# Seven block products accumulated in shared PSUM banks, and layer 1's last MLP quarter in the same form with weight sums formed by adding transfers

## The chip, the cores and the metric

The kernel runs on one core of a Trainium2 chip. The metric is the device time of one execution in microseconds, as the median of several runs. The engines are named as in the profile: PE (TensorE: matmuls; its weight loads stand as PEld), DVE (VectorE), ACT (ScalarE), POOL (GpSimd) and SP (SyncE, which here only issues transfers).

## The reference

Two layers over 512 tokens of width 1024 in float32. Each has three sub-layers of the form x <- LayerNorm(alpha * x + f(x)): a token mixer (mLSTM in layer 0, causal pooling in layer 1), cross-attention into 256 memory tokens, and the MLP, which is what the change touches:

```python
def sq_relu_mlp(x, w1, b1, w2, b2):
    return jnp.square(jax.nn.relu(x @ w1 + b1)) @ w2 + b2      # 1024 -> 4096 -> 1024

for i in range(DEPTH):                                          # DEPTH = 2
    ...
    x = layer_norm(ALPHA * x + sq_relu_mlp(x, mlp_w1[i], mlp_b1[i], mlp_w2[i], mlp_b2[i]),
                   ln_g[i, 2], ln_b[i, 2])
```

## The kernel before

Every float32 operand of a matmul is split in two parts, a high one (a cast on ACT to the format that PE takes) and a low one (the rest, a subtraction on DVE); a product is three matmuls, high by high, high by low and low by high (`mm3`, L196 to L199). Tiles of weights are 128x1024 (512 KB); a matmul is 128x512.

The MLP goes through its 4096 hidden units in four quarters q of 1024. A quarter has a hidden phase (8 tiles of 128 hidden units, 24 matmuls each, then bias, relu and square on ACT) and a down-projection that adds to x, which lies in SBUF as four tiles of 128 tokens by 1024.

For q = 0, 1, 2 (`up_down`) the down-projection is a 2x2 block product by seven products instead of eight. The squared activations are four blocks: a11, a12 for tokens 0 to 255 and a21, a22 for tokens 256 to 511, where the second figure says which half of the quarter's hidden units (a11 and a21 are hidden tiles 0 to 3, a12 and a22 tiles 4 to 7). The weights are b11, b12, b21, b22 in the same way. Sums and differences of blocks are made on DVE (`each` L839 for weights; L845, L869, L873 and one more for activations), then split (L777/L778 activations, L786/L787 weights). A product (`product`) is two groups of 12 matmuls, each into its own PSUM bank of 128x512, 24 in all. The order is M1, M7, M5, M2, M6, P3, P4. M1, M5, M6 and M7 are needed in more than one block of the result: `into` gathers them over q = 0, 1, 2 in two SBUF tiles (`sums`; an ACT copy for q = 0, a DVE add at L852 for the others). M2, P3 and P4 are added to x at once (L859).

For q = 3 the product is direct (`down`): 8 groups of 24 matmuls, 192. In the middle of its hidden phase `gather` (L882 to L893) adds the sums to x, with 16 DVE adds of 128x512. In layer 1 each token tile gets its LayerNorm as soon as its second half is added: statistics (L241), aggregate (L246), a square root on ACT, a reciprocal, four scalar_tensor_tensor (L253, L254), and two transfers to the output.

What runs when: the order of instructions on each engine is fixed when the program is built, by the order of the code, the pools' buffers and the framework's scheduling, and each engine takes its own queue in order, waiting where an operand isn't there. All loads of weights go through SP's queue. Those for the seven products go to a pool of six buffers (`rawd`), so a load waits until an earlier tile of the pool is done with. GpSimd has nothing to do after layer 0's mixer.

Of the kernel before, what the change touches and what calls it, by code (L numbers as in the profile page):

```python
# [15 lines left out]
P = 128  # L16
# [27 lines left out]
def trunk(ctx: ExitStack, tc: tile.TileContext, a: dict, out: bass.AP):  # L44
# [151 lines left out]
    def mm3(out_, l, r, start, stop):  # L196
        T.matmul(out_, l[0], r[0], start=start, stop=False)  # L197
        T.matmul(out_, l[0], r[1], start=False, stop=False)  # L198
        T.matmul(out_, l[1], r[0], start=False, stop=stop)  # L199
        if later:  # L200
            tick(3 * max(r[0].shape[-1], 128) / 2400)
# [451 lines left out]
    for i in range(DEPTH):  # L653
# [137 lines left out]
        def product(name, lhs, rhs, evac):  # L791

            for g in range(2):
                ps = acc_p.tile([P, 512], F32, tag="acc", name=f"{name}{g}")
                for k in range(4):
                    w = rhs[k // 2]
                    mm3(ps, tuple(z[:, k, tok(g)] for z in lhs), (w[0][:, k % 2], w[1][:, k % 2]), start=k == 0, stop=k == 3)
                evac(g, ps)

        sums = {}  # L800

        def up_down(q, n):

# [11 lines left out]
            if q == 0:  # L815
# [7 lines left out]
                for z in "ab":  # L823
                    sums[z] = act_p.tile([P, 2, 2, 512], F32, tag="act", name=f"sum{i}{z}")
                sums["M1"], sums["M6"] = sums["a"][:, 0], sums["a"][:, 1]
                sums["M5"], sums["M7"] = sums["b"][:, 0], sums["b"][:, 1]
# [4 lines left out]
            def load(name, hf, j):  # L831
                z = [scoped["rawd"].tile([P, WU], F32, tag="rawd", name=f"{name}{n}{z}") for z in range(2)]
                for w in range(2):
                    ld(z[w], a["w2"][i, q, hf, j + w])
                return z
# [11 lines left out]
            def into(key):  # L847
                def evac(g, ps):
                    if q == 0:
                        A.copy(sums[key][:, g], ps)  # L850
                    else:
                        V.tensor_tensor(sums[key][:, g], sums[key][:, g], ps, ALU.add)  # L852

                return evac

            def onto(row, hf):
                def evac(g, ps):
                    z = x[2 * row + g][:, hf_cols(hf)]
                    V.tensor_tensor(z, z, ps, ALU.add)  # L859

                return evac

            b11 = load("b11", 0, 0)
            product(f"m1{n}", L["M1"], weight_split(f"b11{n}", b11), into("M1"))
            b12, b22 = load("b12", 1, 0), load("b22", 1, 2)
            each(b11, b11, b12, ALU.add)
            each(b12, b12, b22, ALU.add)
            product(f"m7{n}", L["M7"], weight_split(f"t3{n}", b12), into("M7"))
            V.tensor_tensor(a21, a21, a22, ALU.subtract)  # L869
            product(f"m5{n}", split(f"q1{n}", a21), weight_split(f"t1{n}", b11), into("M5"))  # L870
            b21 = load("b21", 0, 2)
            product(f"m2{n}", split(f"a12{n}", a12), weight_split(f"b21{n}", b21), onto(0, 0))
            V.scalar_tensor_tensor(a11, a11, -1.0, a22, ALU.mult, ALU.subtract)  # L873
            each(b11, b11, b22, ALU.add)
            product(f"m6{n}", split(f"q2{n}", a11), weight_split(f"t2{n}", b11), into("M6"))
            V.tensor_tensor(a12, a12, a11, ALU.add)
            product(f"p3{n}", split(f"q4{n}", a12), weight_split(f"b22{n}", b22), onto(0, 1))
            each(b11, b11, b21, ALU.add)
            product(f"p4{n}", split(f"a22{n}", a22), weight_split(f"t4{n}", b11), onto(1, 0))

        def gather():

            for g in range(2):
                u, w, f, m7 = (sums[z][:, g] for z in ("M1", "M6", "M5", "M7"))
                x11, x12, x21, x22 = (x[2 * r + g][:, hf_cols(c)] for r in range(2) for c in range(2))
                V.tensor_tensor(x11, x11, u, ALU.add)
                V.tensor_tensor(u, u, w, ALU.add)
                V.tensor_tensor(x12, x12, f, ALU.add)
                V.tensor_tensor(x12, x12, u, ALU.subtract)
                V.tensor_tensor(u, u, m7, ALU.add)  # L890
                V.tensor_tensor(x21, x21, u, ALU.add)
                V.tensor_tensor(x22, x22, f, ALU.add)
                V.tensor_tensor(x22, x22, u, ALU.subtract)  # L893

        for q in range(3):
            up_down(q, f"{i}{q}")
        enter(**mixing)
# [11 lines left out]
        for q in range(3, 4):  # L909
            n = f"{i}{q}"  # L910
            hid = Act(f"h{n}")
            for m in range(KC):
                if m == 4:
                    gather()
                    if i + 1 < DEPTH:
                        mixer, xnew, xa = pool_setup()
                evh(hid.k(m), m, q, feat_tile(f"h{n}{m}", a["w1"][i, 8 * q + m], xm, aux_p, "aux"), n)
            if i + 1 < DEPTH:
                for z in range(2):
                    for hf in range(2):  # L920
                        for t in down(hid, q, hf, (2 * z, 2 * z + 1), n):
                            mixer(t, x)
                            kv_back(x[t])
                mk[:] = [kv_flat[0:2], kv_flat[2:4]]
                mv[:] = [kv_flat[4:6], kv_flat[6:8]]
                x = xnew
                continue
# [81 lines left out]
```

## Time and profile before

| | |
|---|---|
| median of three runs | 1199.6 us (1199.43 to 1200.04) |
| profiled execution | 1200.49 us |
| its span | 1198.7 us |
| its granted clock | 0.998 on average |
| PE busy | 1187.9 us (99%) |
| DVE busy | 819.4 us (68%) |
| ACT busy | 582.8 us (49%) |
| POOL busy | 18.8 us (2%) |
| transfers | 146.59 MB, 122 GB/s on average |

An engine's busy share is an average over the whole span. Where PE runs without a gap, as for most of this kernel, the others' waits cost nothing; what a change is worth has to be read from the stage in which it lies. The last three stages are layer 1's third quarter's seven products (1065.6 to 1103.7), its last quarter's hidden phase (1103.7 to 1147.2) and its direct down-projection (1147.2 to 1190.9), after which DVE finishes the LayerNorm of the last 128 tokens.

### The profile page before, as it was taken

The page shows a single profiled execution, that of the slowest core. Times are in us where ns is not written, and L with a number is a line of the kernel's source. Part 1 is how long each engine was busy: PE and PEld are TensorE (multiplying, and loading weights), DVE is VectorE, ACT ScalarE, POOL GpSimd, SP SyncE. Part 2 cuts the span into 40 slices and gives each one's busy share as a digit, 9 for nine tenths or more (in the row PEclk, how much of TensorE's full clock was granted, in tenths as well). Part 3 has the DMA queues.
Part 4 walks back from the last instruction along what each step waited for, and adds up shares of the span by engine and source line. Part 5 has one row for each costly group of instructions (what it writes and reads, how often), then busy time and mean ns, then how long its engine had stood idle before and what let it go on. Part 6 is the DMA issues. An engine that isn't in the chain of part 4 may idle for free.

```text
span 1198.7 us, 15411 instructions
## 1 busy us (share of the span) xinstructions
PE 1187.9 (99%) x6105; PEld 1014.1 (85%) x6105; DVE 819.4 (68%) x1105; ACT 582.8 (49%) x848; POOL 18.8 (2%) x51
## 2 busy tenths in 40 slices
PE   9999999999999999999999999999999999999997
PEld 7888899889888988888888889998888888888886
DVE  6764466585549684594797599874968459479536
ACT  6685774224423564554545444562356445454520
POOL 0211000000000000000000000000000000000000
PEclk9999999999999999999999999999999999999999
DMA  7244247633243326125116455634232512412311
GB/s 273 93 136 123 89 155 267 199 100 106 71 165 99 107 60 187 53 71 175 36 51 208 147 193 178 193 106 175 88 106 80 166 53 83 164 36 61 115 53 71
DMA packets 44057, 146.59 MB, mean 122 GB/s; under 512 B 5568, under 2 KB 5836, under 8 KB 43984
## 3 DMA queue, kind: packets, MB, share of 16 engines
q1 hardware_dynamic: 42960, 142.96, 37.3%
q0 software_dynamic: 1024, 2.64, 0.9%
q8 instruction: 48, 0.79, 0.3%
q14 instruction: 25, 0.20, 0.1%
HBM read 139.27 MB, written 6.31 MB: 121 GB/s over the span
## 4 chain that ended last, share of the span: by engine, by line
PE 95%; DVE 2%; ACT 1%; DMA 1%; issue 0%; SPq 0%; DVEq 0%; ACTq 0%
PE h L198 10%; PE h L197 10%; PE h L199 10%; PE m L197 7%; PE m L199 7%; PE m L198 7%; PE ao L197 2%; PE ao L199 2%; PE ao L198 2%; PE q L197 2%; PE q L198 2%; PE q L199 2%; PE p L197 2%; PE p L199 2%; PE p L198 2%; PE o L197 1%
## 5 line engine op out<-in xcount | busy, mean ns | idle before, releaser
L161 DVE TENSOR_TENSOR wl<-raw,wh 128x1024 fp32r<-128x1024 f32 x175 | 213.0, 1221 | 172.0 <-ACT wh L160 169.7
L160 ACT CAST wh<-raw 128x1024 fp32r<-128x1024 f32 x175 | 183.1, 1048 | 274.5 <-PE h L198 72.6
L839 DVE TENSOR_TENSOR b<-b,b 128x1024 f32<-128x1024 f32 x48 | 58.6, 1220 | 0.4
L197 PE MATMUL h<-xm00h,wh 128*128 128x512 f32 (+1 forms) x144 | 52.8, 367 | 0.0
L197 PE MATMUL h<-xm01h,wh 128*128 128x512 f32 (+1 forms) x144 | 52.8, 367 | 0.0
L197 PE MATMUL h<-xm10h,wh 128*128 128x512 f32 (+1 forms) x144 | 52.8, 367 | 0.0
L197 PE MATMUL h<-xm11h,wh 128*128 128x512 f32 (+1 forms) x144 | 52.8, 367 | 0.0
L198 PE MATMUL h<-xm10l,wh 128*128 128x512 f32 (+1 forms) x144 | 52.7, 366 | 0.0
L198 PE MATMUL h<-xm00l,wh 128*128 128x512 f32 (+1 forms) x144 | 52.7, 366 | 0.0
L199 PE MATMUL h<-xm11h,wl 128*128 128x512 f32 (+1 forms) x144 | 52.6, 365 | 0.0
L199 PE MATMUL h<-xm00h,wl 128*128 128x512 f32 (+1 forms) x144 | 52.6, 365 | 0.0
L199 PE MATMUL h<-xm01h,wl 128*128 128x512 f32 (+1 forms) x144 | 52.6, 365 | 0.0
L198 PE MATMUL h<-xm01l,wh 128*128 128x512 f32 (+1 forms) x144 | 52.6, 365 | 0.0
L198 PE MATMUL h<-xm11l,wh 128*128 128x512 f32 (+1 forms) x144 | 52.6, 365 | 0.0
L199 PE MATMUL h<-xm10h,wl 128*128 128x512 f32 (+1 forms) x144 | 52.6, 365 | 0.0
L248 ACT ACTIVATE rs<-mv,eps_t 128x1 f32<-128x1 f32 x24 | 7.1, 295 | 53.3 <-DVE mv L246 53.3
L811 ACT ACTIVATE r<-h,b 128x512 f32<-128x512 f32 x48 | 32.8, 683 | 0.0
L812 ACT ACTIVATE s<-r 128x512 f32<-128x512 f32 x48 | 30.3, 632 | 1.3
L198 PEld LDWEIGHTS h<-xm00l,wh 128*128 128x128 f32 x144 | 27.2, 189 | 4.5
L198 PEld LDWEIGHTS h<-xm01l,wh 128*128 128x128 f32 x144 | 27.2, 189 | 4.4
L197 PEld LDWEIGHTS h<-xm10h,wh 128*128 128x128 f32 x144 | 27.2, 189 | 4.4
L198 PEld LDWEIGHTS h<-xm10l,wh 128*128 128x128 f32 x144 | 27.1, 189 | 4.4
(934 smaller groups left out, 3513.2 us busy)
## 6 DMA issues: line engine op xcount, KB each, us to landing
raw<-in_w SPq DMA_DIRECT2D x88, 512.0 KB, 4.1
b<-in_w SPq DMA_DIRECT2D x48, 512.0 KB, 4.3
raw<-in_w_q SPq DMA_DIRECT2D x24, 512.0 KB, 4.3
raw<-in_w_ao SPq DMA_DIRECT2D x16, 512.0 KB, 3.7
raw<-in_w_v SPq DMA_DIRECT2D x8, 512.0 KB, 6.0
raw<-in_w_o SPq DMA_DIRECT2D x8, 512.0 KB, 4.3
raw<-in_w_k SPq DMA_DIRECT2D x8, 512.0 KB, 4.5
raw<-in_w_kvv SPq DMA_DIRECT2D x8, 512.0 KB, 5.1
```

The costliest lines, as they stand in the source:

```text
L160: A.copy(h, r)
L161: V.tensor_tensor(l, r, f32(h), ALU.subtract)
L197: T.matmul(out_, l[0], r[0], start=start, stop=False)
L198: T.matmul(out_, l[0], r[1], start=False, stop=False)
L199: T.matmul(out_, l[1], r[0], start=False, stop=stop)
L248: A.activation(rs, mv[:, 1:2], AF.Sqrt, bias=eps_t, scale=1.0)
L811: A.activation(r, ps, AF.Relu, bias=b1[:, i, 8 * q + m : 8 * q + m + 1], scale=1.0)
L812: A.activation(s[m // 4][:, m % 4], r, AF.Square)
L839: V.tensor_tensor(d, u, v, op)
```

## The change

In all quarters that have seven products, these follow each other in six PSUM banks: u (two banks, one for each half of the 256 tokens of a row of blocks), f (two) and m2 (two, from another pool). A product that continues a bank adds to what is there, and x takes the bank's content after each: M1 in u (x11 += u), M5 in f (x22 += f), M6 on top of u (x12 -= u), M2 in m2 (x11 += m2), M7 on top of u (x22 -= u), P3 on top of f (x12 += f), P4 on top of u (x21 += u). The SBUF sums, `into` and `gather` go; M5 instead of M7 is the second product.

In layer 1 the last quarter too is seven products, 168 matmuls in place of 192. There the weight sums t1 = b11 + b12, t2 = t1 + b22, t3 = b12 + b22 and t4 = t2 + b21 are not made on DVE: a plain load brings the first term, and GpSimd issues transfers that add the others to it as they arrive (`onto_w`, ten of 512 KB). t2 and t4 share a tile in another pool. The LayerNorm of tokens 0 to 255 is finished ahead of the last product, that of tokens 256 to 511 after it. Layer 0's last quarter remains direct.

```diff
+    def mm3(out_, l, r, start, stop, skip=False):
...
-        def product(name, lhs, rhs, evac):
+        def product(ps, lhs, rhs, start, evac):
 
             for g in range(2):
-                ps = acc_p.tile([P, 512], F32, tag="acc", name=f"{name}{g}")
                 for k in range(4):
                     w = rhs[k // 2]
...
+                    mm3(ps[g], tuple(z[:, k, tok(g)] for z in lhs), (w[0][:, k % 2], w[1][:, k % 2]), start=start and k == 0, stop=k == 3, skip=not start)
+                evac(g, ps[g])
...
+            def onto(row, hf, op=ALU.add, last=False):
                 def evac(g, ps):
                     z = x[2 * row + g][:, hf_cols(hf)]
-                    V.tensor_tensor(z, z, ps, ALU.add)
+                    V.tensor_tensor(z, z, ps, op)
+                    if last:
+                        ln.stat(2 * row + g, hf, x[2 * row + g])
...
+            u, f, m2 = banks("u", acc_p, "acc"), banks("f", acc_p, "acc"), banks("m2", tmp_p, "tmp")
+            if q < 3:
+                b11 = load("b11", 0, 0)
+                product(u, L["M1"], weight_split(f"b11{n}", b11), True, onto(0, 0))
+                b12 = act_p.tile([P, 2, WU], F32, tag="act", name=f"b12{n}")
+                b12 = load("b12", 1, 0, [b12[:, w] for w in range(2)])
+                each(b11, b11, b12, ALU.add)
+                V.tensor_tensor(a21, a21, a22, ALU.subtract)
+                product(f, split(f"q1{n}", a21), weight_split(f"t1{n}", b11), True, onto(1, 1))
...
+            def onto_w(z, hf, j):
+
+                for w in range(2):
+                    G.dma_start(z[w], a["w2"][i, q, hf, j + w], accum_op=ALU.add)
+
+            def finish(t):
+                ln.finish(t, x[t])
+                for z in range(2):
+                    ld(out[tok(t), hf_cols(z)], x[t][:, hf_cols(z)])
+
             b11 = load("b11", 0, 0)
...
+            product(u, L["M1"], weight_split(f"b11{n}", b11), True, onto(0, 0))
+            t1 = load("t1", 0, 0)
+            onto_w(t1, 1, 0)
+            t2_ = act_p.tile([P, 2, WU], F32, tag="act", name=f"t2{n}")
+            t2_ = load("t2", 0, 0, [t2_[:, w] for w in range(2)])
+            onto_w(t2_, 1, 0)
+            onto_w(t2_, 1, 2)
             V.tensor_tensor(a21, a21, a22, ALU.subtract)
...
+            product(f, split(f"q1{n}", a21), weight_split(f"t1{n}", t1), True, onto(1, 1))
...
+            product(u, L["M7"], weight_split(f"t3{n}", t3), False, onto(1, 1, ALU.subtract, True))
+            w = weight_split(f"t4{n}", t2_)
+            finish(0)
+            finish(1)
+            product(u, s22, w, False, onto(1, 0, last=True))
+            finish(2)
+            finish(3)
```

PE's queue where the second product of layer 1's third quarter begins. Before (M7; m_9249 is M1's second bank, t312 the weight sum, q312 the activation difference a11 - a21; h and l are the high and low part):

```order
L199 MATMUL m_9249<-b1112h_9231,a1112l 128x512
L197 MATMUL m_9283<-t312h_9275,q312h 128x512
L198 MATMUL m_9283<-t312l_9276,q312h 128x512
L199 MATMUL m_9283<-t312h_9275,q312l 128x512
L197 MATMUL m_9283<-t312h_9275,q312h 128x512
```

After (M5; u_9159 is M1's second bank, f_9160 and f_9161 are M5's two, q112 is a21 - a22):

```order
L199 MATMUL u_9159<-b1112h_9172,a1112l 128x512
L197 MATMUL f_9160<-t112h_9212,q112h 128x512
L198 MATMUL f_9160<-t112l_9213,q112h 128x512
L197 MATMUL f_9161<-t112h_9212,q112h 128x512
L198 MATMUL f_9161<-t112l_9213,q112h 128x512
L199 MATMUL f_9160<-t112h_9212,q112l 128x512
```

The second product is now the one whose left operand needs the last hidden tiles, and the first matmuls of its two banks stand ahead of the first one that takes the low part.

ACT's queue at the end of the last quarter's hidden phase in layer 1. Before (wh are weight casts, each waiting for a load on SP's queue; rows at L755 to L759 are a hidden tile):

```order
L160 CAST wh_9870<-raw_9868 128x1024 [waits DMAHW6_49,DVE_49,PE_49]
L755 ACTIVATE r_9807<-h_9782,b_985 128x512 [waits DVE_49,PE_49]
L757 ACTIVATE s_9809<-r_9807 128x512 [waits Activation_49]
L759 ACTIVATE h131h<-r_9807 128x512
L160 CAST wh_9984<-raw_9982 128x1024 [waits DMAHW7_49,PE_49]
L755 ACTIVATE r_9844<-h_9819,b_985 128x512 [waits DVE_49,PE_49]
L757 ACTIVATE s_9846<-r_9844 128x512 [waits Activation_49]
L759 ACTIVATE h131h<-r_9844 128x512
L160 CAST wh_9990<-raw_9988 128x1024 [waits DMAHW0_49,PE_49]
```

After (t113 and t213 are t1 and t2 of this quarter; DMASW are GpSimd's transfers; the last relu and square are those of h_9703):

```order
L786 CAST t113h_9793<-t_9775 128x1024 [waits DMASW4_49,PE_49]
L809 ACTIVATE r_9660<-h_9635,b_985 128x512 [waits PE_49]
L810 ACTIVATE s_9449<-r_9660 128x512 [waits Activation_49]
L786 CAST t113h_9797<-t_9776 128x1024 [waits DMASW5_49,PE_49]
L809 ACTIVATE r_9694<-h_9669,b_985 128x512 [waits PE_49]
L810 ACTIVATE s_9449<-r_9694 128x512 [waits Activation_49]
L786 CAST t213h_9828<-t_9781 128x1024 [waits DMASW0_49,PE_49]
L809 ACTIVATE r_9728<-h_9703,b_985 128x512 [waits PE_49]
L810 ACTIVATE s_9449<-r_9728 128x512 [waits Activation_49]
L777 CAST q113h<-s_9448 128x1024 [waits DVE_49]
```

Casts of t1's two halves and of t2's first half, which wait for GpSimd's transfers, now stand between the hidden tiles, the last of them ahead of the last tile's relu.

DVE's queue at the end of the program. Before (m_10123 is the last group; xp_6476 the last 128 tokens of x):

```order
L254 SCALAR_TENSOR_TENSOR xp_6382<-xp_6382,rr_10115,b_7626 128x512
L767 TENSOR_TENSOR xp_6476<-xp_6476,m_10123 128x512
L241 BN_STATS st_7631<-xp_6476 128x6
L246 BN_AGGR mv_10150<-st_7631 128x2
L253 SCALAR_TENSOR_TENSOR xp_6476<-xp_6476,mv_10150,g_7620 128x512
L250 RECIPROCAL rr_10154<-rs_10152 128x1
L253 SCALAR_TENSOR_TENSOR xp_6476<-xp_6476,mv_10150,g_7622 128x512
L254 SCALAR_TENSOR_TENSOR xp_6476<-xp_6476,rr_10154,b_7624 128x512
L254 SCALAR_TENSOR_TENSOR xp_6476<-xp_6476,rr_10154,b_7626 128x512
```

After (u_9731 and u_9732 hold the last product; xp_6036 are tokens 128 to 255, xp_6337 and xp_6431 the last two tiles):

```order
L253 SCALAR_TENSOR_TENSOR xp_6036<-xp_6036,mv_10023,g_7575 128x512
L253 SCALAR_TENSOR_TENSOR xp_6036<-xp_6036,mv_10023,g_7577 128x512
L254 SCALAR_TENSOR_TENSOR xp_6036<-xp_6036,rr_10027,b_7579 128x512
L254 SCALAR_TENSOR_TENSOR xp_6036<-xp_6036,rr_10027,b_7581 128x512
L845 TENSOR_TENSOR xp_6337<-xp_6337,u_9731 128x512
L845 TENSOR_TENSOR xp_6431<-xp_6431,u_9732 128x512
L241 BN_STATS st_7585<-xp_6337 128x6
L241 BN_STATS st_7586<-xp_6431 128x6
L246 BN_AGGR mv_10063<-st_7585 128x2
L246 BN_AGGR mv_10075<-st_7586 128x2
L253 SCALAR_TENSOR_TENSOR xp_6337<-xp_6337,mv_10063,g_7575 128x512
L250 RECIPROCAL rr_10067<-rs_10065 128x1
```

Two token tiles in place of one are finished behind the last product, and the finish of a tile of the first row of blocks stands directly ahead of its adds.

## Rows read from the trace of the kernel before

**Rows 1.** The page, part 1: busy us of each engine, share of the span, instructions.
```profile
PE 1187.9 (99%) x6105; PEld 1014.1 (85%) x6105; DVE 819.4 (68%) x1105; ACT 582.8 (49%) x848; POOL 18.8 (2%) x51
```
**Rows 2.** Waits of PE, its longest first: engine, line, releaser: us, times, longest.
```profile
PE warm L311 <- POOL zero L308: 1.3, 1, 1.3
PE po L199 <- DVE d1l L207: 1.1, 1, 1.1
PE po L197 <- ACT d1h L206: 0.2, 1, 0.2
```
**Rows 3.** Busy time by stretch, with granted clock (PEclk), DMA share, GB/s.
```profile
1065.80:1103.90 38.10, 38.10 (x169) 31.54 (x169) 36.91 (x39) 19.12 (x20) 0.00 (x0) 1.00 0.06 17
1103.90:1147.40 43.50, 43.50 (x193) 36.03 (x192) 25.29 (x33) 21.84 (x31) 0.00 (x0) 1.00 0.43 131
1147.40:1190.90 43.50, 43.50 (x192) 35.67 (x191) 24.21 (x37) 6.62 (x10) 0.00 (x0) 1.00 0.12 43
...
1194.00:1195.00 1.00, 0.00 (x0) 0.00 (x0) 1.00 (x3) 0.00 (x0) 0.00 (x0) 0.61 0.00 0
743.00:747.00 4.00, 2.71 (x21) 2.37 (x20) 4.00 (x9) 0.58 (x2) 0.00 (x0) 1.00 0.03 12
```
**Rows 4.** PE's timeline at the starts of stages: start us, length, line, operation.
```profile
1022.10 0.39 PE L197 MATMUL h<-xm10h,wh 128*128 128x512 f32 x1
1065.62 0.39 PE L197 MATMUL m<-b1112h,a1112h 128*128 128x512 f32 x1
1103.70 0.39 PE L197 MATMUL h<-xm10h,wh 128*128 128x512 f32 x1
1147.22 0.39 PE L197 MATMUL m<-wh,h130h 128*128 128x512 f32 x1
1190.51 0.39 PE L199 MATMUL m<-wh,h131l 128*128 128x512 f32 x1
```
**Rows 5.** DVE's timeline at the end of the program.
```profile
1190.94 0.69 DVE L767 TENSOR_TENSOR xp<-xp,m 128x512 f32<-128x512 f32 x1 [0.94 <-PE m L199]
1191.66 0.69 DVE L241 BATCH_NORM_STATS2 st<-xp 128x6 f32<-128x512 f32 x1
1192.39 0.21 DVE L246 BATCH_NORM_AGGREGATE mv<-st 128x2 f32<-128x12 f32 x1
1192.63 0.75 DVE L253 SCALAR_TENSOR_TENSOR xp<-xp,mv,g 128x512 f32<-128x512 f32 x1
1193.30 0.16 DVE L250 RECIPROCAL rr<-rs 128x1 f32<-128x1 f32 x1
1193.37 0.73 DVE L253 SCALAR_TENSOR_TENSOR xp<-xp,mv,g 128x512 f32<-128x512 f32 x1
1194.02 1.41 DVE L254 SCALAR_TENSOR_TENSOR xp<-xp,rr,b 128x512 f32<-128x512 f32 x2
```
**Rows 6.** DVE's timeline at the start of the third quarter's products.
```profile
1067.92 1.23 DVE L869 TENSOR_TENSOR s<-s,s 128x1024 f32<-128x1024 f32 x1
1069.06 0.68 DVE L852 TENSOR_TENSOR sum1a<-sum1a,m 128x512 f32<-128x512 f32 x1
1069.66 1.22 DVE L873 SCALAR_TENSOR_TENSOR s<-s,s 128x1024 f32<-128x1024 f32 x1
1070.80 1.22 DVE L778 TENSOR_TENSOR q112l<-s,q112h 128x1024 fp32r<-128x1024 f32 x1
```
**Rows 7.** ACT's timeline in the third quarter: b11's second cast; the last square.
```profile
1049.27 1.05 ACT L786 CAST b1112h<-b 128x1024 fp32r<-128x1024 f32 x1 [2.06 <-PE h L198]
...
1067.26 0.63 ACT L812 ACTIVATE s<-r 128x512 f32<-128x512 f32 x1
```
**Rows 8.** Timelines of DVE, then PE, where a matmul waited for a split.
```profile
43.20 1.21 DVE L161 TENSOR_TENSOR wl<-raw,wh 128x1024 fp32r<-128x1024 f32 x1
...
44.46 0.50 PE L199 MATMUL qk<-x00h,wl 128*128 128x512 f32 x1 [0.19 <-DVE wl L161]
44.80 0.40 PE L197 MATMUL qk<-x00h,wh 128*128 128x512 f32 x1
```
**Rows 9.** DMA issues: destination, engine, count, KB each, median us to landing.
```profile
b<-in_w SPq DMA_DIRECT2D x48, 512.0 KB, 4.3
...
w<-rows POOLq DMA_DIRECT2D x4, 256.0 KB, 3.5
...
w<-rows POOLq DMA_DIRECT2D x4, 64.0 KB, 3.3
```
**Rows 10.** POOL's timeline at two loads issued one behind the other.
```profile
48.34 1.11 POOL L391 DMA_DIRECT2D w<-rows  x2
51.91 0.59 POOL L392 TENSOR_SCALAR_AFFINE_SELECT w<-w 128x128 f32<-128x128 f32 x1 [2.46 <-DMA w<-rows]
52.65 0.29 POOL L392 TENSOR_SCALAR_AFFINE_SELECT w<-w 128x128 f32<-128x128 f32 x1
```

More of the change, by code (lines that the diff above doesn't have):

```diff
@@ L822, in up_down @@
                     V.scalar_tensor_tensor(x[t], x[t], ALPHA, b2, ALU.mult, ALU.add)
[L823 to L826, printed above, removed]
             a11, a21 = s[0][:, :, :256], s[0][:, :, 256:]
@@ L829, in up_down, with load @@
             L, R = {}, {}
-            def load(name, hf, j):
-                z = [scoped["rawd"].tile([P, WU], F32, tag="rawd", name=f"{name}{n}{z}") for z in range(2)]
+            def load(name, hf, j, z=None):
+                z = z or [scoped["rawd"].tile([P, WU], F32, tag="rawd", name=f"{name}{n}{z}") for z in range(2)]
                 for w in range(2):
@@ L863, in up_down @@
-            b11 = load("b11", 0, 0)
[L864 to L868, printed above, removed]
-            V.tensor_tensor(a21, a21, a22, ALU.subtract)
-            product(f"m5{n}", split(f"q1{n}", a21), weight_split(f"t1{n}", b11), into("M5"))
+                    V.tensor_tensor(z, z, ps, op)
@@ new lines, in evac, with banks @@
+                    if last:
+                        ln.stat(2 * row + g, hf, x[2 * row + g])
+                return evac
+            def banks(name, p, tag):
+                return [p.tile([P, 512], F32, tag=tag, name=f"{name}{n}{g}") for g in range(2)]
+            u, f, m2 = banks("u", acc_p, "acc"), banks("f", acc_p, "acc"), banks("m2", tmp_p, "tmp")
[7 more added lines that the diff above has]
+                product(f, split(f"q1{n}", a21), weight_split(f"t1{n}", b11), True, onto(1, 1))
+                b22 = load("b22", 1, 2)
+                V.scalar_tensor_tensor(a11, a11, -1.0, a22, ALU.mult, ALU.subtract)
+                each(b11, b11, b22, ALU.add)
+                product(u, split(f"q2{n}", a11), weight_split(f"t2{n}", b11), False, onto(0, 1, ALU.subtract))
+                b21 = load("b21", 0, 2)
+                product(m2, split(f"a12{n}", a12), weight_split(f"b21{n}", b21), True, onto(0, 0))
+                each(b12, b12, b22, ALU.add)
+                product(u, L["M7"], weight_split(f"t3{n}", b12), False, onto(1, 1, ALU.subtract))
+                V.tensor_tensor(a12, a12, a11, ALU.add)
+                product(f, split(f"q4{n}", a12), weight_split(f"b22{n}", b22), False, onto(0, 1))
+                each(b11, b11, b21, ALU.add)
+                product(u, split(f"a22{n}", a22), weight_split(f"t4{n}", b11), False, onto(1, 0))
+                return
@@ L871, in up_down @@
+            b22 = load("b22", 1, 2)
+            product(u, split(f"q2{n}", a11), w, False, onto(0, 1, ALU.subtract))
             b21 = load("b21", 0, 2)
[L872 to L875, printed above, removed]
+            s12 = split(f"a12{n}", a12)
@@ L876, in up_down @@
             V.tensor_tensor(a12, a12, a11, ALU.add)
[L877 to L893, printed above, removed]
@@ L895, in trunk @@
-        for q in range(3):
+            product(f, split(f"q4{n}", a12), weight_split(f"b22{n}", b22), False, onto(0, 1, last=True))
+            t3 = load("t3", 1, 0)
+            onto_w(t3, 1, 2)
+            product(m2, s12, weight_split(f"b21{n}", b21), True, onto(0, 0, last=True))
+            s22 = split(f"a22{n}", a22)
+            product(u, L["M7"], weight_split(f"t3{n}", t3), False, onto(1, 1, ALU.subtract, True))
+            w = weight_split(f"t4{n}", t2_)
+            finish(0)
+            finish(1)
```

50 lines of the change are left out of this document (18 added, 32 removed).

## The prediction

> **What bounds the kernel now.** I read the busy time by engine first. TensorE (PE) is busy 99% of the span [rows 1], and the table of PE's waits is the check on that: over the program its longest wait is 1.3 us, most are 0.2 us [rows 2]. So wherever PE is the limit, a microsecond of its work is a microsecond of the kernel. Next I read the last 130 us stage by stage [rows 3]. VectorE (DVE) is 36.91 of 38.10 us busy in the seven products of layer 1's third quarter (q=2), but only 25.29 of 43.50 in the next hidden phase and 24.21 of 43.50 in the direct down-projection that ends the kernel. So seven products are the one stage where PE and DVE are limits almost together. The last quarter's down-projection is about to become such a stage and to carry the last LayerNorm as well. Last I read the end: PE's last matmul starts at 1190.51 [rows 4], and DVE then works until 1195.43 (1194.02 + 1.41) on the last 128 tokens [rows 5]: add, statistics, four scalar_tensor_tensor (STT).
>
> The profiled execution took 1200.49 us with a span of 1198.7; the median of the three runs is 1199.6. I work out a difference within the profiled execution and add it to 1199.6.
>
> **1. Layer 1's last quarter: 24 matmuls fewer, on PE.** The direct form is 8 groups of 24, 192 matmuls, in 43.50 us [rows 3]: 0.2266 each. Seven products are 7 x 24 = 168. PE work falls by 24 x 0.2266 = **5.4 us**. That is the gain if PE remains the limit to the end.
>
> **2. The same stage on DVE.** Let S' = 1147.22 be where the down-projection's first matmul starts [rows 4]. In q=2 the corresponding moment is S = 1065.62, and DVE starts the subtraction of the activations at 1067.92, S + 2.30 [rows 6]; it can't be sooner, since the square of the last hidden tile ends on ACT at 1067.89, S + 2.27 [rows 7]. From there on the changed kernel has in DVE's queue, until its end: 17 operations of 128x1024 (splits and activation sums), 14 PSUM adds of 128x512, 8 BN statistics, 16 STT, 4 aggregates and 4 reciprocals. By the distance of starts in a full queue: 1.14 (1069.66 to 1070.80), 0.60 (1069.06 to 1069.66) [rows 6], 0.66 for an STT (1192.63 to 1193.30), 0.24 + 0.07 for an aggregate and a reciprocal (1192.39 to 1192.63, 1193.30 to 1193.37) [rows 5]. A statistic stands 0.73 ahead of what depends on it [rows 5]; here other work follows it, so I take it between an add and that, 0.65. The sum is 19.4 + 8.4 + 5.2 + 10.6 + 1.2 = 44.8 us, so DVE ends at S' + 2.3 + 44.8 + 0.1 = S' + 47.2 = 1194.4, if it never idles. Before, it ended at 1195.43. The gain at the end of the program is therefore **1.0 us** (0.3 with 0.4 us of idling and 0.73 for the statistics, 1.8 with 0.60 for all small ones), not 5.4. PE's last product would end some 8 us earlier than DVE. The order of DVE's queue shows the same: the four STT of tokens 128 to 255 stand ahead of the last product's adds, and eight STT behind them.
>
> **3. The six other quarters: M5 comes second.** Before, the second product was M7, with operands from the first hidden half, which are long done; now it is M5, with q1 = a21 - a22, which needs the last hidden tile. The first matmul that needs its low part q1l is M5's fifth (two matmuls of each bank go ahead), due at S + (24 + 4) x 0.2266 = S + 6.35. In q=2 DVE wrote q1l from 1070.80 for 1.22 us, to S + 6.40 [rows 6], and the same five operations stand ahead of it after the change. So PE waits 0.05 us for data plus the restart: where PE waited for a split that ended at 44.41, the matmul started at 44.46 and the next one at 44.80 instead of 0.23 later [rows 8], about 0.16 us more. I take 0.2 us a quarter, **1.2 us** in six, added to a stretch where PE is the limit. Bounds: 0.05 and 0.35 a quarter, 0.3 and 2.1 in all.
>
> **4. What costs nothing.** The 16 adds of the old gather (16 x 0.60 = 9.6 us) lay in hidden phases where DVE has 18 us free [rows 3]; taking them out gives nothing. The adds into x replace adds into the sums one for one, except in q=0, where ACT's eight copies become DVE adds; that makes q=0 what q=1 and q=2 were, and these run with PE full. A bank returns after two or more products (over 10.9 us) while its add is due within about 3 us of the product's end, so reuse of banks hides unless DVE falls far behind.
>
> **5. The weight sums by adding transfers.** These decide. In the order of ACT, the cast of t2's first half stands ahead of the last hidden tile's relu and square, and of q1's cast: whoever waits for that sum holds back everything in part 2. It is due when the relu is, H0 + 43.49, with H0 = 1103.70 [rows 4]; every microsecond behind that is a delay D of DVE's whole chain, one for one, and of M5 on PE.
> When can the sum be there? Its base load is issued by SP behind b21's, which waits for the buffer that b11's second split frees. That split's cast started at 1049.27 in q=2 [rows 7], whose hidden phase began at 1022.10 [rows 4]: H0 + 27.17, then 1.05 for the cast and 1.22 for the split, H0 + 29.5. Two issues later the load goes out at H0 + 29.9 and lands after 4.3 us [rows 9], H0 + 34.2. Then GpSimd adds b12, waits, adds b22, which must land before the cast: two transfers one behind the other, each A from issue to landing. D = 34.3 + 2A - 43.5 = 2A - 9.2.
> No row of before shows an adding transfer. From below: a plain GpSimd load took 3.3 us for 64 KB and 3.5 for 256 KB [rows 9], so 512 KB would take 3.8 by the same slope. From above: the old contents are read and the sum written one after the other, twice that, 7.6. In this stretch there are neighbours too (the hidden weights, 131 GB/s on average [rows 3], and t3's own loads and sums in the same queue). I take the middle, A = 5.7, since nothing draws it to either end: **D = 2.2 us**; the bounds give 0 and 6.0.
> The Trainium skill, in "DMA: Bandwidth & Descriptors", section "Anatomy of one DMA — SWDGE (gpsimd) path", puts a transfer at about 2.0 us plus bytes at 436 GB/s, which is 3.2 us for 512 KB; "Collectives: The Full Stack", section "The bandwidth ceiling: the fold count and why AG ≠ RS ≠ AR", says that an add reads two sources and so runs at half the rate. As an estimate from both pages that is 4.4 us, and D would be 0: the sums come in time. The row for 256 KB, 3.5 us, is above the first rule's 2.6.
>
> **The sum:** -1.0 + 1.2 + 2.2 = +2.4 us, 1199.6 + 2.4 = **1202.0**.
>
> **Rivals.**
> *Sums in time* (A under 4.6): D = 0, and what is left is -1.0 + 1.2 = +0.2, 1199.8 (1198.1 to 1201.4). For it: the plain loads' 3.5 us; against it: the addition needs a second stream of 512 KB, and the bound of 4.6 leaves 0.8 us for it. (The pages of the Trainium skill named above lead here.) 0.27.
> *Sums much later:* each adding transfer behind the one ahead of it in GpSimd's queue, three ahead of the cast instead of two (t2's other half is issued in between), each at 5.7: D = 3 x 5.7 - 9.2 = 7.9, less what of M1 and of the splits is done meanwhile, and with PE idle for over 3 us perhaps a lower clock: it stayed at 1.00, the upper level (2.4 GHz), through a wait of 1.1 us between 743 and 747 [rows 2, 3], but the microsecond from 1194.0, 3.1 us after the last matmul's end, shows 0.61 [rows 3], on its way to the lower (1.2 GHz). It decides from D = 4: 1204 to 1209, slower. For it: ten such transfers on one queue. Against: of two loads issued there at 48.34, 0.55 us apart, the first was waited for 2.46 us by the next operation and the second not again [rows 10]. 0.19.
> *PE remains the limit to the end* (the side of faster): if DVE has the STT of tokens 0 to 255 done before the last product ends, and D = 0, the 5.4 us appear on PE, less what two token tiles behind the end take over one: 8.5 us for two adds, two statistics, two aggregates and reciprocals and eight STT, against 4.5 [rows 5]. That leaves a gain of 1.4; with no loss in the six quarters, 1198.2, which reaches under 1197.2 only if the tail is 1 us shorter too. Against it: the 44.8 us of part 2. 0.06.
> *It doesn't do what it says:* the second product's late operand is absorbed in the six quarters, because q1l has its cast earlier; 1.2 us drop out of the sum: 1200.8, inside the forecast's own range, so it gets no chance of its own.
>
> **How the numbers follow.** Forecast case (D between 1 and 4, the bounds of parts 2 and 3): 1202.0, 1200.3 to 1204.5, chance 0.48. The rivals have 0.27, 0.19 and 0.06. About 0.2% (2.4 us) is what a measurement can tell here: faster is under 1197.2, slower over 1202.0. Slower: half the forecast case and all of the late one, 0.24 + 0.19 = 0.43. Faster: most of the 0.06, 0.05, since no case's centre lies there. The rest, 0.52, is the same. The range that leaves out no more than 2 in 10 goes from 1198.2 (most of the sums in time) to 1206.5 (half of the late case).
>
> **What would show it.** Parts 1 and 2: in the last stage of the changed kernel DVE busy nearly throughout, PE with gaps, and over 8 us between PE's last matmul and DVE's last STT (4.5 before). Part 3: a PE wait of about 0.2 us on the DVE split of q1, once in each of six quarters. Part 5: ACT waiting for an adding transfer ahead of the last relu, by D; the transfers' time from issue to landing is A. I am wrong if A is under 4.6, if PE's gaps in the last stage are small, or if the quarters q=0 to 2 grow by more than 0.35 us each.

## The result

The changed kernel takes 1206.84 us in the median (1205.37 to 1209.23), beside 1200.16 for the kernel before on the same chip: ratio 1.0058, 95% interval 1.0048 to 1.0068. It is slower, by 6.7 us. The forecast was a loss of 2.4 us, 1202.0, with a range from 1198.2 to 1206.5; "no change" had a chance of 0.52, "slower" 0.43. The loss is almost three times as large as the sum said.

The profiled execution took 1206.08 us with a span of 1204.3. Page, part 1, of the changed kernel, which answers to [rows 1]:

```profile
PE 1185.2 (98%) x6081; PEld 1009.6 (84%) x6081; DVE 827.9 (69%) x1104; ACT 584.3 (49%) x837; POOL 28.0 (2%) x61
```

PE has 24 matmuls fewer and is busy for 2.7 us less, and yet the span is 5.6 us longer. The table of PE's waits says where PE now stops (engine, line, releaser: us in total, times, longest):

```profile
PE f L197 <- ACT q113h L777: 4.3, 1, 4.3
PE warm L311 <- POOL zero L308: 1.3, 1, 1.3
PE po L199 <- DVE d1l L207: 1.1, 1, 1.1
PE po L197 <- ACT d1h L206: 1.0, 1, 1.0
```

The first of them is new. It is the second product (M5) of layer 1's last quarter, waiting for the cast of q1. ACT's timeline shows what kept that cast (start, length, and in brackets the idle time before and what ended it):

```profile
1145.15 0.63 ACT L810 ACTIVATE s<-r 128x512 f32<-128x512 f32 x1
1154.17 1.05 ACT L786 CAST t213h<-t 128x1024 fp32r<-128x1024 f32 x1 [8.39 <-DMA t<-in_w]
1155.12 0.68 ACT L809 ACTIVATE r<-h,b 128x512 f32<-128x512 f32 x1
1155.84 0.63 ACT L810 ACTIVATE s<-r 128x512 f32<-128x512 f32 x1
1157.76 1.05 ACT L777 CAST q113h<-s 128x1024 fp32r<-128x1024 f32 x1 [1.29 <-DVE s L895]
```

ACT sat idle for 8.39 us ahead of the cast of t2's first half, and the last hidden tile's relu stood behind it. By PE's timeline the hidden phase began at 1105.43 and the products at 1148.95, so that cast was due at 1148.92, and the relu 0.95 behind it. They came at 1154.17 and 1155.12, 5.25 us late. DVE, which answers to [rows 5, 6], then worked through its queue:

```profile
1155.25 1.23 DVE L787 TENSOR_TENSOR t213l<-t,t213h 128x1024 fp32r<-128x1024 f32 x1 [9.46 <-ACT t213h L786]
1156.50 1.23 DVE L895 TENSOR_TENSOR s<-s,s 128x1024 f32<-128x1024 f32 x1
...
1193.15 1.28 DVE L845 TENSOR_TENSOR xp<-xp,u 128x512 f32<-128x512 f32 x2
...
1199.87 1.41 DVE L254 SCALAR_TENSOR_TENSOR xp<-xp,rr,b 128x512 f32<-128x512 f32 x2
```

The subtraction of L895, due 2.3 us after the stage's start, at 1151.25, came 5.25 us late; from there to DVE's end at 1201.28 it is 44.78 us. These rows give the account of the profiled difference. DVE ended at 1195.43 before and at 1201.28 now, 5.85 us later: the last hidden phase began 1.73 us later (1105.43, against 1103.70 in [rows 4]), the sum came 5.25 late, and the stage from its start to DVE's end is 1.13 shorter without that delay (2.3 + 44.78 against 1195.43 - 1147.22 = 48.21).

The transfers that made the sum late, in GpSimd's timeline; t2's first half gets b12 at 1140.22 and b22 at 1147.88:

```profile
1140.22 0.89 POOL L880 DMA_DIRECT2D t<-in_w  x1 [39.84 <-DMA t<-in_w]
1141.91 0.88 POOL L880 DMA_DIRECT2D t<-in_w  x1 [0.80 <-DMA t<-in_w]
1147.88 1.76 POOL L880 DMA_DIRECT2D t<-in_w  x2 [5.09 <-DMA t<-in_w]
```

The base load had landed 34.8 us into the phase (34.3 was forecast). The first add took until 1147.88, 7.7 us, and the second until the cast at 1154.17, 6.3 us: 13.95 us together, where 11.4 was forecast.

### The profile page after: what moved, and what is told of

It reads as the page before. It is cut to its first block, busy times and chain, and to the rows that moved or that the text cites. A ratio compares the mean times of both kernels' runs of the same rounds, so it can differ in the third digit from the quotient of the medians.

```text
span 1204.3 us, 15369 instructions
## 1 busy us (share of the span) xinstructions
PE 1185.2 (98%) x6081; PEld 1009.6 (84%) x6081; DVE 827.9 (69%) x1104; ACT 584.3 (49%) x837; POOL 28.0 (2%) x61
## 4 chain that ended last, share of the span: by engine, by line
PE 90%; DVE 5%; DMA 2%; ACT 1%; issue 1%; SPq 0%; POOL 0%; DVEq 0%; ACTq 0%; POOLq 0%
PE h L198 9%; PE h L197 9%; PE h L199 9%; PE u L199 4%; PE u L198 4%; PE u L197 4%; PE ao L197 2%; PE ao L199 2%; PE ao L198 2%; PE q L197 2%; PE q L198 2%; PE q L199 2%; PE f L199 2%; PE m L199 2%; PE f L197 2%; PE m L198 2%
## 5 line engine op out<-in xcount | busy, mean ns | idle before, releaser
L161 DVE TENSOR_TENSOR wl<-raw,wh 128x1024 fp32r<-128x1024 f32 x167 | 203.5, 1221 | 182.8 <-ACT wh L160 178.2
L160 ACT CAST wh<-raw 128x1024 fp32r<-128x1024 f32 x167 | 174.9, 1050 | 261.5 <-PE h L198 76.0
L809 ACT ACTIVATE r<-h,b 128x512 f32<-128x512 f32 x56 | 38.3, 683 | 14.8 <-PE h L199 14.8
L810 ACT ACTIVATE s<-r 128x512 f32<-128x512 f32 x56 | 35.5, 634 | 1.7
L880 POOL DMA_DIRECT2D t<-in_w x10 | 8.9, 911 | 1039.0 <-DMA t<-in_w 1030.5
```

The source lines that it names most:

```text
L160: A.copy(h, r)
L161: V.tensor_tensor(l, r, f32(h), ALU.subtract)
L809: A.activation(r, ps, AF.Relu, bias=b1[:, i, 8 * q + m : 8 * q + m + 1], scale=1.0)
L810: A.activation(s[m // 4][:, m % 4], r, AF.Square)
L880: G.dma_start(z[w], a["w2"][i, q, hf, j + w], accum_op=ALU.add)
```

## The experiments

**The sum early, and M5's low part late.** Two kernels on the changed one, then the same for the part of the change outside the last quarter. In `early_t2` the tile, the load and the first four adds of t2 move from behind t1's to ahead of the quarter's hidden phase, which lets SP and GpSimd start them in the quarter before:

```diff
+            if q == 3:
+                t2_ = act_p.tile([P, 2, WU], F32, tag="act", name=f"t2{n}")
+                ...
+                for hf, j in ((1, 0), (1, 2)):
+                    for w in range(2):
+                        G.dma_start(t2_[w], a["w2"][i, q, hf, j + w], accum_op=ALU.add)
             s = [act_p.tile([P, 4, S], F32, tag="act", name=f"s{n}{b}") for b in range(2)]
...
```

> The changed kernel with t2's tile, base load and its first four adding transfers written ahead of the last quarter's hidden phase; nothing else differs. Theory (the sum t2 comes late, ACT's cast of it holds back the last relu by about 6 us, and DVE then works 44.8 us without a gap): ACT no longer waits there, DVE's end lies 44.8 us behind the subtraction at S' + 2.3, and the time falls by 5 to 6 us, to 1200.5 to 1201.8. Rival (the adding transfers are slow wherever they stand and hold back t1, t3 or the weights of the hidden phase, or the last stage is long for another reason): 1204 or more.

Measured: 1199.83 us (1198.83 to 1201.64), ratio to the kernel before 1.000 (0.9991 to 1.0009). The loss is gone, 7.0 us of the medians, a little more than the 5 to 6 that were expected. In its timeline ACT takes the cast and the relu on time:

```profile
1147.79 1.05 ACT L786 CAST t213h<-t 128x1024 fp32r<-128x1024 f32 x1 [3.14 <-PE h L198]
1148.75 0.68 ACT L817 ACTIVATE r<-h,b 128x512 f32<-128x512 f32 x1
```

The wait now ends with PE. DVE's subtraction, and its last operation:

```profile
1150.13 1.23 DVE L899 TENSOR_TENSOR s<-s,s 128x1024 f32<-128x1024 f32 x1
...
1192.89 1.41 DVE L254 SCALAR_TENSOR_TENSOR xp<-xp,rr,b 128x512 f32<-128x512 f32 x2
```

The stage that began at 1147.82 ends on DVE 46.5 us later, at 1194.30. Between the two profiled executions DVE's end differs by 6.98 us. The delay of the subtraction is 5.25 of it, and 0.6 is DVE's work behind it, with 0.5 us more of waits for PE in the changed kernel. The other 1.13 lie ahead of the last hidden phase (it begins at 1104.30 here), where PE's waits for d1h and d1l between the layers are 0.5 us here and 2.1 in the changed kernel; these waits differ by nearly as much between kernels that are alike there (see part 4 below), so nothing shows that part to be this edit's.

In `early_lows`, M5 in addition takes its matmuls with q1's low part last in each bank (z = 0 in the cut takes the high part's matmuls, z = 1 the low part's):

```diff
+                if lows:
+                    for z in range(2):
+                        for k in range(4):
...
+                    evac(g, ps[g])
+                    continue
```

> As early_t2, and in M5 the matmuls that take q1's low part stand last in each bank, so that it is due 0.9 us later. Theory (0.25 us lost in each of six quarters, since q1's low part comes just too late): M5 takes 5.44 us again, PE reaches the last hidden phase 1.5 us earlier, and the time is 1.5 us under early_t2, 1199.0 to 1200.3. Rival (the 0.25 us is a price of the bank's continuation or of DVE being behind, which moves to the next product): the same time as early_t2.

Measured: 1198.28 us (1197.08 to 1200.23), ratio 0.9983 (0.9974 to 0.9992): 1.55 us under `early_t2`. PE's timeline at M5 in the first quarter, of the changed kernel, from the fourth matmul on, and then of `early_lows`, where the last row is the first with the low part:

```profile
430.30 0.39 PE L198 MATMUL f<-t100l,q100h 128*128 128x512 f32 x1
430.63 0.50 PE L199 MATMUL f<-t100h,q100l 128*128 128x512 f32 x1
430.97 0.40 PE L197 MATMUL f<-t100h,q100h 128*128 128x512 f32 x1
```

```profile
431.34 0.39 PE L800 MATMUL f<-t100h,q100h 128*128 128x512 f32 x1
431.57 0.39 PE L801 MATMUL f<-t100l,q100h 128*128 128x512 f32 x1
431.80 0.39 PE L803 MATMUL f<-t100h,q100l 128*128 128x512 f32 x1
```

The fifth matmul came 0.33 after the fourth in place of 0.23, and the next one 0.34 after it: 0.2 us that the table of waits doesn't list, and the starts of M5 and of the product behind it are 5.68 to 5.70 us apart in place of 5.44. In `early_lows` the low matmul follows at the usual 0.23.

`direct_last` gives layer 1's last quarter back its direct form, without adding transfers; `direct_lows` has M5's low matmuls last as well.

```diff
-        for q in range(3 if i + 1 < DEPTH else 4):
+        for q in range(3):
             up_down(q, f"{i}{q}")
-        if i + 1 == DEPTH:
-            break
...
```

> The changed kernel with layer 1's last quarter in the direct form of the kernel before, without GpSimd's transfers: the part of the change in the six other quarters alone. Theory: 6 x 0.25 = 1.5 us slower than the kernel before, 1201.7, and 0.75 us more if the longer wait of PE on d1h between the layers belongs to the change, 1202.4. Rival (adds in shared banks cost nothing and the 1.7 us at the start of the last hidden phase are chance): 1200.2.

> As direct_last, with M5's low matmuls last in each bank. Theory: the 1.5 us go, 1200.2 to 1201.0, the same as the kernel before. Rival (the loss has another cause than q1's low part): the same time as direct_last.

Measured: 1202.29 us, ratio 1.0017 (1.0008 to 1.0026), and 1200.76, ratio 1.0004 (0.9995 to 1.0013). `direct_last` lies between its two expected times, 1201.7 and 1202.4. The shared banks as such show neither cost nor gain (the interval of `direct_lows` is 0.6 us less to 1.6 us more); M5 in second place costs 1.53 us here and 1.55 above. All four kernels ran on one chip, so the seven products in the last quarter are worth the difference of `early_lows` and `direct_lows`, 1198.28 against 1200.76: 2.5 us, where PE has 5.4 us less to do.

**What makes an adding transfer long.** `plain_adds` has the same ten transfers at the same places without the addition, so that each overwrites its tile and the weight sums of the last quarter are left out.

```diff
-                    G.dma_start(z[w], a["w2"][i, q, hf, j + w], accum_op=ALU.add)
+                    G.dma_start(z[w], a["w2"][i, q, hf, j + w])
```

> The changed kernel with GpSimd's ten transfers as plain loads that overwrite their tile (the weight sums of layer 1's last quarter are left out); same queue, same sizes, same places. Theory (the add itself makes a transfer long): they take 3.5 to 4.5 us from issue to landing in place of 6.1 to 9.5, t2 is in time, and the kernel takes about 1200. Rival (GpSimd's issue or the neighbours in that stretch make them long, not the add): 6 us or more, and 1205.

Measured, one run: 1202.28 us. Neither expectation held: the time lies in the middle between 1200 and 1205, and so do the three transfers shown below. ACT's cast of t2's first half in `plain_adds`:

```profile
1150.98 1.05 ACT L786 CAST t213h<-t 128x1024 fp32r<-128x1024 f32 x1 [4.83 <-DMA t<-in_w]
```

It was due at 1149.29, 43.49 us behind the hidden phase's start at 1105.80, so it was still 1.7 us late: two plain transfers, one behind the other, took 10.1 us there, where the two adds took 13.95. The answers on transfers (destination, queue, count, KB, us from issue to landing), for the issues at 1140.22, 1141.91 and 1147.88 of the changed kernel, where the last covers the first of two:

```profile
t<-in_w POOLq DMA_DIRECT2D x1, 512.0 KB, 7.3
...
t<-in_w POOLq DMA_DIRECT2D x1, 512.0 KB, 8.2
...
t<-in_w POOLq DMA_DIRECT2D x1, 512.0 KB, 6.2
```

and for those at 1140.88, 1141.86 and 1145.86 of `plain_adds`:

```profile
t<-in_w POOLq DMA_DIRECT2D x1, 512.0 KB, 4.6
...
t<-in_w POOLq DMA_DIRECT2D x1, 512.0 KB, 5.4
...
t<-in_w POOLq DMA_DIRECT2D x1, 512.0 KB, 5.1
```

With the addition gone from all ten, a transfer is 1.1 to 2.8 us shorter there. An add's price depends on company: in `early_t2`, t2's second pair of adds, issued at 1055.48 and 1057.96 with no load beside them, took

```profile
t<-in_w POOLq DMA_DIRECT2D x1, 512.0 KB, 5.4
...
t<-in_w POOLq DMA_DIRECT2D x1, 512.0 KB, 5.6
```

although the second was issued before the first had landed; t1's two, issued at 1095.62 and 1097.97 beside the loads for the next phase, took 9.4 and 10.9. In the changed kernel SP issued t3's two loads at 1140.37 and 1145.82, in the midst of t2's adds. `early_t2` tells a little of which neighbour counts. Two of its adds were issued at 1150.84 and 1151.45 with no load beside them; they took

```profile
t<-in_w POOLq DMA_DIRECT2D x1, 512.0 KB, 5.5
...
t<-in_w POOLq DMA_DIRECT2D x1, 512.0 KB, 8.3
```

So the second of a close pair takes longer and the first does not (5.7 and 7.2 for the pair issued at 1049.42 and 1050.33), and t2's other half, issued second, is not what made the first add of the changed kernel 7.3 us long. Beside that add were also the loads on SP's queue. From 1140.3 to 1147.4 (queue, packets, MB, share of the DMA engines' time; q0 is GpSimd's queue, q1 SP's):

```profile
q0 software_dynamic: 177, 0.66, 49.5%
q1 hardware_dynamic: 164, 0.56, 39.3%
```

That is by elimination; no run moves these loads alone, and in `early_t2` an add issued at 1143.15, with one load of t3 issued 1.5 us behind it, took 5.5 us.

What the engines do in the stretch from 1141 to 1147, in the changed kernel and then in `plain_adds` (busy us of PE, PEld, DVE, ACT, POOL, then PE's clock, the DMA engines' busy share, GB/s):

```profile
1141.00:1147.00 6.00, 6.00 (x28) 4.97 (x27) 1.23 (x1) 2.27 (x3) 0.99 (x2) 1.00 0.97 185
```

```profile
1141.00:1147.00 6.00, 6.00 (x28) 4.99 (x27) 1.23 (x1) 2.27 (x3) 1.98 (x4) 1.00 0.74 262
```

With the adds the DMA engines are busy 0.97 of the time at 185 GB/s; without them they move 262 at a share of 0.74. Busy share per GB/s is 1.86 times as high, though nearly half of the bytes in the changed kernel's row (0.53 of 1.11 MB) are plain loads on SP's queue. GpSimd's queue over the whole execution gives the ten transfers by themselves (packets, MB, share of the span; the kernel before, which has none of them, then the changed kernel, then `plain_adds`):

```profile
q0 software_dynamic: 1024, 2.64, 0.9%
q0 software_dynamic: 2464, 7.89, 3.2%
q0 software_dynamic: 2464, 7.89, 2.2%
```

They keep the engines busy for 2.3% of the span with the addition and 1.3% without, about 1.8 times as long. The Trainium skill, "Collectives: The Full Stack", section "The bandwidth ceiling: the fold count and why AG ≠ RS ≠ AR", says of the reduce step of a ring that its add reads two sources and so halves the rate: these rows come near that. The 4.4 us that was worked out from it and the Trainium skill's "DMA: Bandwidth & Descriptors" does not agree: 5.4 us was the shortest.

**The cast later in the queue.** `cast_late` leaves the transfers where they are and queues t2's casts and splits behind q1's on ACT and DVE (`at` holds q1's cast and split).

```diff
-            w = weight_split(f"t2{n}", t2_)
+            with tc.issue_after(at[0].ins), tc.issue_after(at[1].ins):
+                w = weight_split(f"t2{n}", t2_)
```

> The changed kernel with t2's casts and splits queued behind q1's on ACT and DVE; the transfers and all else stay where they are. Theory (what costs is that the cast of a late sum stands ahead of the last relu; M6, which needs t2, is due 11 us after the stage's start, and t2's first half came 5 us after it): the relu is on time, M5 follows M1 at once, and 4 to 6 us of the loss go, 1201 to 1203, with DVE waiting a little for t2's second half. Rival (the sums are so late that M6 waits as long as the relu did): 1205 or more.

Measured: 1205.79 us, ratio 1.0043 (1.0028 to 1.0058); the rival held. By the profile of its slowest run, 1208.01, the relu came on time and M5 followed M1 without a gap, as expected, but the next product, M6, paid. ACT and DVE in `cast_late`:

```profile
1161.08 1.04 ACT L788 CAST t213h<-t 128x1024 fp32r<-128x1024 f32 x1 [5.23 <-DMA t<-in_w]
```

```profile
1162.15 1.23 DVE L789 TENSOR_TENSOR t213l<-t,t213h 128x1024 fp32r<-128x1024 f32 x1 [4.45 <-ACT t213h L788]
```

t2's second half, whose last add was issued at 1151.61 and took 9.4 us, held back ACT's cast of q2 behind it and M6 on PE, and DVE sat idle for 4.45 us. So the place of the cast was not the cause by itself: the sum's second half was late for its own user too, which I had not priced.

**Whose queue sets the end.** `dve_sums` makes the last quarter's weight sums on DVE, as in the other quarters, and has no adding transfers.

> Layer 1's last quarter as seven products with its weight sums on DVE, as in the other quarters, without GpSimd's transfers. In DVE's queue only t4's two sums stand behind the subtraction a21 - a22; the other six lie in the hidden phase, where DVE is free. Theory (DVE's queue sets the end of the last stage): 2 x 1.14 = 2.3 us more than with t2 early, 1201.5 to 1202.8. Rival (PE or the loads set the end there, so two more DVE operations hide): as early_t2, 1200.

Measured: 1202.72 us, ratio 1.0028 (1.0016 to 1.0040). By its timeline the subtraction came on time (2.31 us after the stage's start at 1148.44) and DVE ended at 1197.66, 46.91 us after it; in `early_t2` it is 44.17. Two operations of 1.14 explain 2.3 of the 2.7 us. PE runs without a gap in both kernels, 38.13 us from the stage's start to its last matmul. So more work in DVE's queue costs its full length here.

Is less of it then a gain? `off01` takes the finish of tokens 0 to 255 from DVE: ACT multiplies by the reciprocal and adds a bias, GpSimd multiplies by g and adds b.

```diff
+                A.activation(y, y, AF.Identity, bias=nm, scale=rr)
+                G.tensor_tensor(y, y, self.g[hf], ALU.mult)
+                G.tensor_tensor(y, y, self.b[hf], ALU.add)
```

> As early_lows, and the LayerNorm of tokens 0 to 255 in the last stage is finished on ACT (x times reciprocal plus a bias) and GpSimd (times g, plus b) in place of eight scalar_tensor_tensor on DVE. Theory (DVE's queue sets the end, those eight stand ahead of the last product's adds): the first half of the last product is added while PE works on the second, and only one token tile is left behind the last matmul as in the kernel before; 1.5 to 2.5 us less than early_lows, 1195.8 to 1196.8. Rival (GpSimd slows DVE beside it, or its own chain of eight operations ends last): 1198 or more.

Measured: 1200.50 us, ratio 1.0001 (0.9992 to 1.0010), slower than `early_lows`. DVE took the first half of the last product earlier, as meant, but GpSimd slowed it. DVE and then POOL in `off01`:

```profile
1189.45 1.14 DVE L254 SCALAR_TENSOR_TENSOR xp<-xp,rr,b 128x512 f32<-128x512 f32 x1
...
1190.74 1.51 DVE L253 SCALAR_TENSOR_TENSOR xp<-xp,mv,g 128x512 f32<-128x512 f32 x1
...
1192.25 0.73 DVE L253 SCALAR_TENSOR_TENSOR xp<-xp,mv,g 128x512 f32<-128x512 f32 x1
```

```profile
1190.12 1.59 POOL L270 TENSOR_TENSOR xp<-xp,b 128x512 f32<-128x512 f32 x1
```

The same operation takes 1.14 to 1.67 us while GpSimd computes and 0.73 after; five of the eight behind the last product are longer by 3.0 us together. The adds from PSUM keep their 0.68. The Trainium skill, "SBUF — State Buffer", section "Who interferes with whom", says that a DVE instruction with two inputs in SBUF contends with a GpSimd instruction that reads SBUF, and one with at most one SBUF input, outside DVE's 2-port modes, does not: these rows agree.

`actstat` moves only the statistics of tokens 0 to 255, to ACT, as two passes with an accumulated sum:

```diff
+            A.activation(junk, x, AF.Copy, scale=1.0 / 1024, accum_out=m1)
+            A.activation(junk, x, AF.Square, scale=1.0 / 32, accum_out=m2)
```

> As early_lows, and the statistics of tokens 0 to 255 in the last stage are made on ACT, which is idle there (a sum and a sum of squares over 1024 columns each), in place of four BN statistics and two aggregates on DVE. Theory (DVE's queue sets the end, and the first half of the last product waits for it): DVE has 2.5 us less ahead of the last product's adds, less what it waits for ACT's sums; 1.0 to 2.5 us under early_lows, 1195.8 to 1197.3. Rival (the 8 us of work behind PE's last matmul set the end, whatever stands ahead): within 0.5 us of early_lows, 1198.

Measured: 1197.81 us (1196.06 to 1198.27), ratio 0.9981 (0.9972 to 0.9990), which can't be told from `early_lows` at 0.9983. The rival held. PE's last matmul in `early_lows` and in `actstat`:

```profile
1185.26 0.39 PE L199 MATMUL u<-t413h,a2213l 128*128 128x512 f32 x1
```

```profile
1185.01 0.39 PE L199 MATMUL u<-t413h,a2213l 128*128 128x512 f32 x1
```

From the stage's start (1147.39 and 1147.14) that is 37.87 us in both, without a gap, against 43.29 in the kernel before [rows 4]. DVE ends 8.4 us behind it in `early_lows` and 8.1 in `actstat`, against 4.9 in the kernel before: two token tiles in place of one are finished there. So DVE's end moved by 0.3 us against the stage's start, and most of the 2.5 us went into waits of DVE, as its timeline in `actstat` shows:

```profile
1174.33 1.23 DVE L804 TENSOR_TENSOR t413l<-t,t413h 128x1024 fp32r<-128x1024 f32 x1 [1.23 <-ACT t413h L803]
...
1176.56 0.22 DVE L263 SCALAR_TENSOR_TENSOR nv<-mv 128x1 f32<-128x1 f32 x1 [0.41 <-ACT junk L262]
```

With that much taken off, DVE waits for a cast of t4 on ACT, which waited 3.07 us for PE's M2, and for ACT's sums. In `early_lows`, then, two limits end within 0.3 us of each other: DVE's queue, and PE's work with the two tiles behind it. More work in the queue costs in full (`dve_sums`), less brings 0.3. `early_lows` and `actstat` beat both kernels, by 0.17% and 0.19% against the kernel before.

## Why the prediction was wrong

**Part 1, 24 matmuls on PE: right in size.** From the stage's start to its last matmul PE takes 37.87 us in `early_lows` and 43.29 in the kernel before, 5.4 less. That the end doesn't gain as much was right too: 3.4 us go to the second token tile behind the last matmul, and 2.0 are left by the rows, 2.5 by the medians.

**Part 2, DVE's queue as the new limit: right that it is full, but not the only limit.** 44.8 us from the subtraction to the end were forecast and 44.78 measured in the changed kernel. That close a match is luck: 0.7 us of it are waits for PE, and `early_t2`, with 0.2 us of them, has 44.17. Statistics took 0.60 apart in a full queue, not 0.65, and the finish of two tiles interleaves. The bounds given with it, gains of 0.3 and 1.8, can't be worked out from the terms named for them (0.64 for the statistics and 0.4 of idling leave nothing of the 1.0). The gain of the stage was forecast as 1.0 us. It is 1.1 in the changed kernel and 2.0 in `early_lows` (from its stage's start at 1147.39 to 1193.62, 46.2, against 48.2). PE's last matmul started at 1192.93, 8.35 us ahead of DVE's end; over 8 was the mark. The other mark, PE with gaps, was a poor one, although small gaps were named as a sign of being wrong: in `early_t2` and `early_lows` DVE is full and PE has no gap in the stage at all. DVE's surplus shows only behind PE's last matmul.

**Part 3, M5 second: right.** 1.2 us forecast, six times 0.25 = 1.5 measured, 1.53 and 1.55 by the two pairs of kernels.

**Part 4, what costs nothing: right as far as a run can tell**, by `direct_lows` at 1.0004. The 0.75 us that PE waited longer for d1h between the layers need not be the change's: the pair of waits for d1h and d1l is 1.3 in the kernel before, 2.1 in the changed one, and 0.5 to 1.8 in the nine others, whose code between the layers is the changed kernel's.

**Part 5, the adding transfers: this step failed.** The chain was right: which cast waits, what stands behind it, and that each microsecond counts in full. What was wrong is the size of D, and in it of A, the time of one add: 5.7 us taken as the middle of 3.8 and 7.6, and 7.3 and 6.2 measured from issue to landing in that chain. With 0.5 us in all between the landings and what waited for them, which the sum had left out, that is 7.0 a step (7.7 and 6.3). D is twice A less 9.2, so 1.3 us a step became 2.6 us, and with the base load 0.5 us later the delay was 5.25 in place of 2.2. For an add with little beside it the middle was near (5.4 and 5.6), by luck, since nothing drew it to either end. It failed because I had named neighbours, t2's other half and t3, and given them no price, although the loads of t3 and both halves of t2 run at the same time. By `early_t2` t2's other half doesn't lengthen the first add, which leaves the loads on SP's queue; how much each of them adds I have not taken apart, and what made the second add 6.2 stays open: t3's loads, moved away by themselves, would tell.

The medians moved by 6.7 us, 0.8 more than the rows account for, and the runs spread over 3.9 us where those of the kernel before spread over 0.9. The adds' time may vary from run to run, but no profile of a slower run shows it, and 33 runs of the kernel before on another chip spread over 4.1 without any add.

**The rivals.** The time was that of "sums much later" (1204 to 1209), with the price in the wrong place: the adds don't wait for each other's end (those issued at 1140.22 and 1141.91, of 7.3 and 8.2 us, run side by side for over five), they share busy DMA engines. The lower clock that I named in it came too, from 1158.8 on, behind the 4.3 us that PE waited:

```profile
1148.00:1153.00 5.00, 5.00 (x23) 4.13 (x23) 0.00 (x0) 0.00 (x0) 2.52 (x3) 1.00 1.06 256
1158.80:1162.00 3.20, 3.14 (x7) 2.33 (x8) 3.20 (x4) 2.86 (x5) 0.00 (x0) 0.50 1.00 193
```

A clock of 0.50 is the lower level, 1.2 GHz. M5 took 7.07 us from its first matmul to the next product's, against 5.68 elsewhere. It set little, since DVE was 3.20 us busy in those 3.20; behind them DVE waited 0.40 us for M5's first bank, which it doesn't in `early_t2`:

```profile
1163.86 0.69 DVE L845 TENSOR_TENSOR xp<-xp,f 128x512 f32<-128x512 f32 x1 [0.40 <-PE f L199]
```

"Sums in time" was priced at 1199.8; `early_t2`, which makes it true, took 1199.83. It is 0.4 us under the kernel before on its chip, where the rival had 0.2 over, so part of that match is luck.

"PE remains the limit to the end" was priced at 1198.2 for sums in time and no loss in the six quarters. `early_lows` has both and took 1198.28, and its PE has no gap in the stage and a longer tail behind it, as that rival has it, beside a DVE queue that is full as well. The 0.06 was low for a mechanism that a kernel so near this one shows.

## What to carry to other kernels

Where a step is handed from an engine to transfers, put it so early that their time can double, and count every transfer of that kind that is under way with it: here the same code written ahead of the quarter's hidden phase was worth 6 to 7 us. An operation that waits for such a transfer must not stand in its engine's queue ahead of the work that everything else needs, and moving it back helps only if its own user can wait. Work taken off the busiest engine is worth only the distance to the next limit, here 2.0 to 2.5 us of 5.4: look at what the next engine does at the end of that very stage before counting it.

## What the runs showed of the hardware

An adding transfer of 512 KB from HBM into SBUF took 5.4 to 5.9 us in six of ten cases in `early_t2`, with at most one load or add under way beside it for most of its time, 7.2 and 8.3 as the second of two adds issued within 1 us, and 9.4 and 10.9 beside the loads for the next phase; in the changed kernel the ten took 6.1 to 9.5. A plain one on the same queue took 3.7 to 6.1. The ten adds keep the DMA engines busy about 1.8 times as long as ten plain transfers (2.3% and 1.3% of the span). To issue an adding one takes GpSimd 0.89 us, a plain one 0.53. A matmul that starts 0.1 us late for its operand costs about 0.25 us in its product (5.68 to 5.73 for 5.44), which the table of waits doesn't list, and six of these are 1.5 us. A scalar_tensor_tensor of 128x512 on DVE takes 0.73 us, and up to 1.67 while GpSimd computes on SBUF.
